# An 8192 x 8192 transpose in two strips: letting regions fill across the seam between the strips

## The chip, the cores and the metric

The kernel runs on one core of a Trainium2 chip. The metric is the device time of one execution in microseconds (us). Every traced execution took about 1.8 us longer than its span, the time from the first to the last instruction. All comparisons of times use runs of state fast. The runs named "look" are single runs, whose state the record calls unknown; only their traces are used.

## The reference

```python
def setup_inputs():
    return {"x": np.random.randn(8192, 8192).astype(np.float32)}

def reference(x):
    return np.transpose(x)
```

268.44 MB are read and 268.44 MB written. There is no arithmetic.

## The kernel before

The matrix is walked in 128 steps: strip 1 (columns 0 to 4095) in 64 chunks of 128 rows, then strip 2. A step loads one chunk of 128 x 4096 values (2 MB), transposes it in 128 x 128 blocks on TensorE, and copies the blocks from PSUM, where TensorE's results land, into *regions* in SBUF, where loads land and stores start. Loads and stores are DMA transfers; SyncEngine issues them into one queue. The output rows of a strip are divided into eight ranges q of 512 rows, and each range has one region open. A region is stored when it holds eight chunks, so that a row of the store is 8 x 128 values = 4096 B. The ranges are staggered: in each step just one region fills, and 2 MB go out beside 2 MB coming in.

At the end of a strip the stagger is cut off: `min(..., CH - 1)` closes all eight regions in step 63, with 8, 7, ... 1 chunks, and strip 2 starts with eight empty regions, the first of which close with 1, 2, ... 8 chunks.

```python
        for t, (s, c) in enumerate(chunks):
            nc.tensor.wait_ge(s_ld[t % NIN], 16 * (t // NIN + 1))
            closing = []
            for q in [(c + k) % NR for k in range(NR)]:
                if q not in window:
                    end = min(c + (q - c) % W, CH - 1)
                    r = free.pop(0)
                    window[q] = (c, end, r)
                    if stored[r]:
                        (nc.scalar, nc.vector)[q % 2].wait_ge(s_st[r], 16 * stored[r])
                ...      # four transposes, one copy, by ScalarE (q even) or VectorE (q odd)
                if c == end:
                    closing.append((q, e, copied[e]))
            for q, e, count in closing:
                ...
                nc.sync.wait_ge(s_cp[e], count)
                ...      # one store of 512 rows on SyncEngine's queue
                st.then_inc(s_st[r], 16)
                free.append(r)
            if t + NIN < len(chunks):
                nc.sync.wait_ge(s_pe, n)
                load(t + NIN)      # NIN = 3 input buffers
```

## Time and profile before

| | |
|---|---|
| time, 3 runs | 1265.46 us median (1265.32 to 1265.71) |
| the profiled run | 1266.41 us, span 1264.6 us |
| chain that ended last | 76% waiting for loads to land, 20% transposes |
| loads | 128 of 2 MB, 23.2 us from issue to landing |
| stores | 142: 114 of 2 MB, 28 shorter ones |

### The profile page before, as it was taken

The numbers are of one execution on the slowest core, as the hardware profiler recorded it, in microseconds if no ns is written. First come the engines' busy times: TensorE is split into PE (matmuls) and PEld (weight loads), VectorE is DVE, ScalarE is ACT, GpSimd is POOL, SyncE is SP. The second block draws the span as 40 slices with busy tenths as digits, with TensorE's granted clock in tenths as the row PEclk, the third lists the DMA queues.
The fourth block names the chain that finished last, engine by engine and source line by source line (L and its number), as shares of the span: only waits on it lengthen the run. The fifth ranks groups of instructions, "written<-read, shape, count | busy, mean of one in ns | idle before, by whom it ended". The sixth has DMA issues, their size and how long they took to land.

```text
span 1264.6 us, 9814 instructions
## 1 busy us (share of the span) xinstructions
PE 741.1 (59%) x4096; PEld 714.3 (56%) x4096; DVE 353.5 (28%) x512; ACT 301.1 (24%) x513; POOL 0.7 (0%) x6
## 2 busy tenths in 40 slices
PE   5555655655556565655556665656556655665651
PEld 5555555655556555655445555656456655665551
DVE  3322322322223222232133322223222222232220
ACT  3222222222222222222122222222222222222220
POOL 0000000000000000000000000000000000000000
PEclk9878777777776868687668778686866777767685
DMA  9999999999999999999999999999999999999998
GB/s 385 426 428 428 430 427 430 430 429 429 429 428 429 430 429 429 430 428 429 428 404 421 430 428 429 431 429 429 429 428 430 429 428 429 430 430 430 428 428 354
DMA packets 39308, 537.51 MB, mean 425 GB/s; under 512 B 4320, under 2 KB 4832, under 8 KB 6240
## 3 DMA queue, kind: packets, MB, share of 16 engines
q1 hardware_dynamic: 39264, 536.89, 99.9%
q8 instruction: 32, 0.52, 0.2%
q14 instruction: 12, 0.10, 0.0%
HBM read 268.44 MB, written 268.44 MB: 425 GB/s over the span
## 4 chain that ended last, share of the span: by engine, by line
DMA 78%; PE 20%; issue 0%; DVE 0%; ACT 0%; SPq 0%; ACTq 0%
DMA in<-in_x_dram 76%; PE ps L132 20%; DMA out_dram<-reg 2%; DVE reg L145 0%; ACT reg L143 0%; SPq L198 0%; SPq L69 0%; ACTq L141 0%
## 5 line engine op out<-in xcount | busy, mean ns | idle before, releaser
L132 PE MATMUL ps<-ident,in 128*128 128x128 f32 x4096 | 741.1, 363 | 495.5 <-DMA in<-in_x_dram 480.9
L132 PEld LDWEIGHTS ps<-ident,in 128*128 128x128 f32 x4096 | 714.3, 219 | 522.0 <-DMA in<-in_x_dram 496.4
L145 DVE COPY reg<-ps 128x512 f32<-128x512 f32 x512 | 353.5, 691 | 883.3 <-PE ps L132 849.3
L143 ACT COPY reg<-ps 128x512 f32<-128x512 f32 x512 | 299.8, 586 | 935.2 <-PE ps L132 904.1
L143 ACT ACT_TABLE_LOAD x1 | 1.3, 1283 | 0.9 <-SPq L69 0.9
L84 POOL TENSOR_SCALAR_AFFINE_SELECT ident<-ident 128x128 f32<-128x128 f32 x1 | 0.3, 293 | 0.2 <-POOL ident L82 0.2
L82 POOL MEMSET ident<- 128x128 f32 x1 | 0.2, 205 | 0.5 <-SPq L69 0.5
L187 POOL MEMSET const-bfloat16-1.0<- 128x1 bf16 x1 | 0.1, 102 | 0.0
L187 POOL MEMSET const-uint8-127<- 128x1 uint8 x1 | 0.1, 102 | 0.0
L187 POOL MEMSET const-float32-0.0<- 128x1 f32 x1 | 0.1, 99 | 0.2 <-issue 0.2
L187 POOL MEMSET const-float32-1.0<- 128x1 f32 x1 | 0.1, 99 | 0.0
## 6 DMA issues: line engine op xcount, KB each, us to landing
in<-in_x_dram SPq DMA_DIRECT2D x128, 2048.0 KB, 23.2
out_dram<-reg SPq DMA_DIRECT2D x114, 2048.0 KB, 22.6
out_dram<-reg SPq DMA_DIRECT2D x4, 1792.0 KB, 19.8
out_dram<-reg SPq DMA_DIRECT2D x4, 1536.0 KB, 19.1
out_dram<-reg SPq DMA_DIRECT2D x4, 1280.0 KB, 19.0
out_dram<-reg SPq DMA_DIRECT2D x4, 1024.0 KB, 17.7
out_dram<-reg SPq DMA_DIRECT2D x4, 768.0 KB, 16.1
out_dram<-reg SPq DMA_DIRECT2D x4, 512.0 KB, 14.2
```

The source lines that it names most:

```text
L82: nc.gpsimd.memset(ident, 0.0).then_inc(s_id, 1)
L84: nc.gpsimd.affine_select(out=ident, in_=ident, compare_op=mybir.AluOpType.not_equal, fill=1.0, base=0, pattern=[[-1, P]], channel_multipl ...
L132: last = nc.tensor.transpose(ps[:, b * P:(b + 1) * P], ins[t % NIN][:, q * B * P + b:(q + 1) * B * P - B + b + 1:B], ident,)
L143: cp = nc.scalar.copy(out=o, in_=i)
L145: cp = nc.vector.tensor_copy(out=o, in_=i)
L187: nc = _bacc.Bacc("TRN2", target_bir_lowering=False, num_devices=1)
```

## The change

A range's last chunks of strip 1 and its first chunks of strip 2 share one region. The stagger goes on across step 64. A region that straddles the seam is stored by two DMAs (7+1 chunks, 6+2, ... 1+7), as its two parts lie in different output rows.

```diff
-                    end = min(c + (q - c) % W, CH - 1)
+                    span = (q - c) % W + 1
                     r = free.pop(0)
-                    window[q] = (c, end, r)
+                    parts = [(s, c, min(c + span, CH))]
+                    if c + span > CH and t + span < len(chunks):
+                        parts.append((s + 1, 0, c + span - CH))
+                    window[q] = (t, r, parts)
 ...
-                if c == end:
+                if t + 1 == t0 + sum(z - a for _, a, z in parts):
                     closing.append((q, e, copied[e]))
             for q, e, count in closing:
 ...
                 nc.sync.wait_ge(s_cp[e], count)
+                base = 0
+                for s_, a, z in parts:
+                    ...      # one store for each part, from its place in the region
```

More of the change, by code (lines that the diff above doesn't have):

```diff
@@ L117 @@
                 if q not in window:
-                    end = min(c + (q - c) % W, CH - 1)
+                    span = (q - c) % W + 1
                     r = free.pop(0)
-                    window[q] = (c, end, r)
+                    parts = [(s, c, min(c + span, CH))]
+                    if c + span > CH and t + span < len(chunks):
+                        parts.append((s + 1, 0, c + span - CH))
+                    window[q] = (t, r, parts)
                     if stored[r]:
                         (nc.scalar, nc.vector)[q % 2].wait_ge(s_st[r], 16 * stored[r])
-                c0, end, r = window[q]
-                rows = (end - c0 + 1) * P
-                view = regs[r][:, :B * rows].rearrange("p (b i) -> p b i", b=B)
+                t0, r, parts = window[q]
+                k = [p[0] for p in parts].index(s)
+                base = B * P * sum(z - a for _, a, z in parts[:k])
+                _, a, z = parts[k]
+                rows = (z - a) * P
+                view = regs[r][:, base:base + B * rows].rearrange("p (b i) -> p b i", b=B)
                 ps = pss[n % NPS]
@@ L138 @@
                 n += 1
-                o = view[:, :, (c - c0) * P:(c - c0 + 1) * P]
+                o = view[:, :, (c - a) * P:(c - a + 1) * P]
                 i = ps.rearrange("p (b i) -> p b i", b=B)
@@ L148 @@
                 bank[(n - 1) % NPS] = (s_cp[e], copied[e])
-                if c == end:
+                if t + 1 == t0 + sum(z - a for _, a, z in parts):
                     closing.append((q, e, copied[e]))
             for q, e, count in closing:
-                c0, end, r = window.pop(q)
-                rows = (end - c0 + 1) * P
-                j0 = s * J + q * B * P
-                dst = out[j0:j0 + B * P, c0 * P:c0 * P + rows]
-                dst = dst.rearrange("(q b) i -> q b i", q=P)
-                nc.sync.wait_ge(s_cp[e], count)
-                if stores:
-                    st = wide_dma(nc, nc.sync, "qSPDynamicHW", dst, regs[r][:, :B * rows])
-                else:
-                    st = nc.sync.dma_start(
-                        out=dst, in_=regs[r][:, :B * rows].rearrange("q (b i) -> q b i", b=B)
-                    )
-                st.then_inc(s_st[r], 16)
-                stores += 1
-                stored[r] += 1
+                t0, r, parts = window.pop(q)
+                nc.sync.wait_ge(s_cp[e], count)
+                base = 0
+                for s_, a, z in parts:
+                    rows = (z - a) * P
+                    j0 = s_ * J + q * B * P
+                    dst = out[j0:j0 + B * P, a * P:a * P + rows]
+                    dst = dst.rearrange("(q b) i -> q b i", q=P)
+                    src = regs[r][:, base:base + B * rows]
+                    base += B * rows
+                    if stores:
+                        st = wide_dma(nc, nc.sync, "qSPDynamicHW", dst, src)
+                    else:
+                        st = nc.sync.dma_start(
+                            out=dst, in_=src.rearrange("q (b i) -> q b i", b=B)
+                        )
+                    st.then_inc(s_st[r], 16)
+                    stores += 1
+                    stored[r] += 1
                 free.append(r)
```

## The prediction

> **What bounds the kernel now.** I read the page first: its busy shares, the 40 slices, the chain that ended last.
>
> ```profile
> span 1264.6 us, 9814 instructions
> PE 741.1 (59%) x4096; PEld 714.3 (56%) x4096; DVE 353.5 (28%) x512; ACT 301.1 (24%) x513; POOL 0.7 (0%) x6
> ...
> GB/s 385 426 428 428 430 427 430 430 429 429 429 428 429 430 429 429 430 428 429 428 404 421 430 428 429 431 429 429 429 428 430 429 428 429 430 430 430 428 428 354
> ...
> q1 hardware_dynamic: 39264, 536.89, 99.9%
> ...
> DMA 78%; PE 20%; issue 0%; DVE 0%; ACT 0%; SPq 0%; ACTq 0%
> ```
>
> No compute engine is busy over 59%; the DMA queue is at 99.9%. The slices (31.6 us each) hold 427 to 431 GB/s nearly everywhere. They fall short in four: 385 and 426 at the start, 354 at the end, and 404 and 421 in slices 21 and 22, which is the seam, where strip 1 (steps 0 to 63) gives way to strip 2. The change works on the seam alone. The page prices it: (429-404)/429 x 31.6 + (429-421)/429 x 31.6 = 1.8 + 0.6 = 2.4 us of lost transfer. That is the first estimate of all that is to be had.
>
> Second, the table by windows, cut where the chain shows loads landing: step 63's at 601.72, step 73's at 702.39; then 5 us pieces inside (columns: busy time of each engine, granted TensorE clock, DMA share, GB/s).
>
> ```profile
> 572.44:601.72 29.28, 17.99 (x96) 17.42 (x96) 8.30 (x12) 7.04 (x12) 0.00 (x0) 0.69 1.01 429
> 601.72:702.39 100.67, 56.60 (x320) 51.88 (x320) 27.19 (x40) 23.17 (x40) 0.00 (x0) 0.72 1.01 417
> 702.39:731.68 29.29, 17.39 (x96) 16.82 (x96) 8.30 (x12) 7.03 (x12) 0.00 (x0) 0.74 1.01 429
> ...
> 635.00:640.00 5.00, 2.22 (x8) 1.42 (x8) 0.03 (x1) 0.59 (x1) 0.00 (x0) 0.50 1.02 386
> 640.00:645.00 5.00, 3.38 (x12) 2.18 (x12) 2.66 (x5) 2.09 (x5) 0.00 (x0) 0.50 1.01 401
> 645.00:650.00 5.00, 0.00 (x0) 0.00 (x0) 1.08 (x2) 0.55 (x1) 0.00 (x0) 0.50 1.03 381
> 650.00:655.00 5.00, 4.20 (x20) 4.20 (x21) 1.17 (x2) 1.17 (x2) 0.00 (x0) 0.50 1.02 428
> 655.00:660.00 5.00, 5.00 (x43) 5.00 (x42) 3.58 (x6) 2.64 (x5) 0.00 (x0) 0.98 1.00 406
> 660.00:665.00 5.00, 3.48 (x29) 3.29 (x28) 2.01 (x3) 2.20 (x5) 0.00 (x0) 1.00 1.00 380
> ```
>
> Three steps take 29.28 us on either side, 9.76 us a step. The ten steps across the seam take 100.67 us, 3.1 us over 97.6. In bytes the loss is 100.67 x (1 - 417/429) = 2.8 us. The DMA share stays at 1.00 or over even where the rate is 381: the engines never show as idle, single packets take longer.
>
> Third, why the rate dips: the SyncEngine's timeline, the waits, and the store latencies in steady state (tile view, 100 to 590 us).
>
> ```profile
> 598.34 0.34 SPq L99 DMA_DIRECT2D in<-in_x_dram  x1
> 603.65 30.76 SPq L28 DMA_DIRECT2D out_dram<-reg  x8
> 634.45 3.65 SPq L99 DMA_DIRECT2D in<-in_x_dram  x1
> 638.15 0.59 SPq L28 DMA_DIRECT2D out_dram<-reg  x1
> 638.79 1.99 SPq L99 DMA_DIRECT2D in<-in_x_dram  x1
> ...
> DVE reg L145 <- DMA out_dram<-reg: 34.0, 6, 17.7
> ACT reg L143 <- DMA out_dram<-reg: 31.1, 4, 13.5
> ...
> DMA to landing us min/median/max: 22.5/22.6/24.1
> ```
>
> At step 63 all eight regions close. The first of their stores takes about 0.6 us to issue, like a normal one (0.54); the fourth takes 8.19, because the queue takes no more. So the next load, issued every 9.8 us otherwise, goes out 36 us after the one before, and step 64 has to wait for regions to be stored (65 us of waits on stores in the whole run, 63.5 of them here). When the stall is over the queue holds only the smallest stores: many rows, few bytes. It runs nearly dry.
>
> **What the Trainium skill says.** (1) "DMA: Bandwidth & Descriptors", Specifications, gives a fabric ceiling of 435 GB/s for the 16 engines. The trace agrees: 429 is 98.6% of it, so steady state has nothing left and only the dips can be regained. (2) The same page, Anatomy of one DMA: the DMA engines do not wait on semaphores, the issuing sequencer does, before dispatch. The trace agrees: the load issued at 634.45 stands behind eight stores issued over 30.76 us. (3) The same page, "Why small descriptors are slow (HBM only)": a fixed overhead per packet. The trace's packet records agree in kind: medians of 611 ns for 16384 B, 315 for 8192, 161 for 4096 and 89 for 2048; the slope from 4096 to 16384 is 36.6 ns per 1000 B, which leaves about 12 to 14 ns fixed.
>
> **The change, part by part.** *Removed*: the burst of eight stores in step 63 and the thin stores of 1 to 7 chunks in steps 64 to 70. *Added*: nothing; the instruction order of the built kernel shows the same 4096 transposes, 512 copies, 128 loads and 142 stores with the same sizes. *Moved*: step 63 stores one full region, and each of steps 64 to 70 stores a pair (7+1, 6+2, ... 1+7 chunks), followed by its load. So every step across the seam moves 2 MB in and 2 MB out, as in steady state.
>
> What is regained: I took the packets that run more than 60 ns over that line (14 ns + 36.4 ns per 1000 B), and added up the excess, divided by 16 engines. In the seam they lie in three clusters: at 638.5 us (13 packets, 0.41 us), 642.4 (50, 0.83) and 658.8 (32, 0.75), 2.0 us together. They coincide with the 5 us windows of 386, 401/381 and 406/380 GB/s. The same sort of cluster stands at the kernel's start (1.7, 15.2, 21.6 us), where the queue is thin too; in steady state such packets come singly, worth some 0.03 us every 40 us. I take the clusters to be a queue that ran dry.
>
> What isn't regained: small packets. The 14 short stores stay, with the same rows. Seven full regions as 16 KB packets would take 7 x 128 x 615 ns / 16 = 34.4 us; the same bytes in the short stores take 35.1 us (half of the totals by packet size of the whole run, as each strip end has a mirror at the start and end). So 0.7 us stay. Check: counted from the packet records, 42.08 MB crossed the seam window, which at 429 GB/s takes 98.1 us, a loss of 2.6 us; less 0.7 leaves 1.9. That agrees with the 2.0 of the clusters.
>
> Beside other work: the second store of a pair costs SyncEngine 0.54 us before the load goes out, but the queue then holds over 20 us of transfers (22.6 us from issue to landing), so it is hidden. Sum: 1265.46 - 1.9 = 1263.5 us.
>
> **The rivals.** *A, the stall was on the path with its full length.* The seam shows over 60 us of waits on stores; step 63 to step 66 takes 49 us where 29.3 would be normal. If all that came back, the time would fall by 20 us or more, to 1245 or, with the waits counted whole, near 1202. Against: the same bytes must still go through a queue that stays at 429 GB/s until 625 us, during the stall; the 20 us lost to loads there are spent on stores, and given back afterwards, when steps 64 to 70 store little (step 66 to 73 takes 51.6 us where 68.3 is normal). *B, a new wait takes its place.* A pair is 1024 rows against a full region's 512, so the queue could fill and SyncEngine stall on issue; and a region is free only when both stores have landed. The reuse margin is small: a store issued at 573.88 lands some 22.6 us later, at 596.5, and the copy that reuses such a region starts at 598.4, 1.9 us of slack. For it: issues did stall at the fourth store above. Against: a stall on a full queue starves nobody, since what is in it, pairs and loads of 2 MB each, is many microseconds of work; a late region holds up the last copy of a step by a microsecond, while TensorE idles 3 to 4 us a step. B leaves between 1263.5 and, if the queue still thins somewhere, 1265.5 (no gain). *C, all of the seam's loss returns*, also the 0.7 us, because slow packets behind small ones are hidden in a full queue: 1265.46 - 2.6 to 3.1, so 1262.4 to 1262.9.
>
> **Range and chances.** The central value is 1263.5. C sets the lower end at 1262.4; half of the gain lost to B, with 0.2 us of run to run spread (1265.32 to 1265.71), sets the upper at 1264.7. Two per cent is 25.3 us, ten times what the seam's dips hold; only rival A reaches that, and it contradicts the byte count. Slower by 2% would need a hang-up that nothing shows. Chances: 0.005 faster, 0.99 within 2%, 0.005 slower.
>
> **What would show each step right or wrong.** Right: slices 21 and 22 at 427 or more; no 5 us window of the seam under about 415; no cluster of slow packets from 600 to 710 us; the waits of copies on stores down from 65 us to a few; SyncEngine's issues at the seam as pairs, one load every 9.8 us; ten steps across the seam in about 98.5 us, not 100.67. Start and end slices unchanged (385, 354). Wrong: if the waits vanish and the dips remain, the dips aren't the thin queue but the short rows; if the rate is flat and the span doesn't fall, the loss has moved elsewhere, first to look at the last slice; a fall of over 5 us would mean that the stall itself was on the path.

## The result

The changed kernel took 1265.7 us median (1265.37 to 1265.88, 6 runs) against 1265.39 us (1265.2 to 1265.8, 6 runs) for the kernel before. The ratio is 1.0002, with an interval from 0.9989 to 1.0015. A ratio is the mean time of one kernel's fast runs over that of the other's in the same rounds, so it isn't quite the ratio of the medians quoted. The time is within 2% of before, as predicted, but outside the predicted range (1262.4 to 1264.7): nothing of the expected 1.9 us appeared. Over all batches, the 42 fast runs of before that served as the comparison have a mean of 1265.62 us (standard deviation 0.51; 1265.64 with the five of before_again) and 11 of the changed kernel 1265.66 (0.17). The difference is 0.04 us, with a standard error of 0.51/√42 and 0.17/√11 taken together, 0.09 us.

Yet the profile of the changed kernel shows what the change was for. From its page:

```profile
span 1263.6 us, 9807 instructions
...
GB/s 385 427 427 430 428 427 430 429 430 429 428 428 428 430 429 429 428 430 429 427 427 412 430 429 428 429 429 429 429 429 429 429 429 427 431 429 429 430 427 351
...
DMA 78%; PE 19%; issue 0%; ACT 0%; SPq 0%; ACTq 0%
```

Slice 21 is mended (427 for 404), slice 22 isn't: 412, where before had 421. The table by windows, cut at the same loads (steps 60, 63, 73 and 76), then 5 us pieces near the end of the seam:

```profile
571.98:601.26 29.28, 16.52 (x96) 15.95 (x96) 8.30 (x12) 7.02 (x12) 0.00 (x0) 0.83 1.01 429
601.26:701.60 100.34, 61.19 (x320) 59.29 (x320) 27.66 (x40) 23.43 (x40) 0.00 (x0) 0.71 1.01 423
701.60:730.88 29.28, 16.59 (x96) 16.02 (x96) 8.29 (x12) 7.03 (x12) 0.00 (x0) 0.79 1.01 429
...
680.00:685.00 5.00, 3.68 (x20) 3.68 (x21) 1.38 (x2) 0.83 (x2) 0.00 (x0) 0.66 1.05 423
685.00:690.00 5.00, 1.66 (x14) 1.46 (x13) 1.38 (x2) 1.51 (x3) 0.00 (x0) 1.00 0.95 349
```

The mean rate over the seam rose from 417 to 423 GB/s. But the ten steps take 100.34 us, only 0.33 less than in the kernel before. There is a new dip, 349 GB/s, at 685 us. The waits of the copies on stores are down from 65 us to 1.7:

```profile
ACT reg L150 <- DMA out_dram<-reg: 1.7, 2, 1.1
```

and SyncEngine's timeline shows a wait in a new place (start, duration, issue):

```profile
606.94 0.34 SPq L99 DMA_DIRECT2D in<-in_x_dram  x1
612.85 1.22 SPq L28 DMA_DIRECT2D out_dram<-reg  x2
...
627.26 6.37 SPq L99 DMA_DIRECT2D in<-in_x_dram  x1
633.90 2.92 SPq L28 DMA_DIRECT2D out_dram<-reg  x2
638.10 5.94 SPq L99 DMA_DIRECT2D in<-in_x_dram  x1
...
678.14 4.42 SPq L99 DMA_DIRECT2D in<-in_x_dram  x1
683.21 0.61 SPq L28 DMA_DIRECT2D out_dram<-reg  x1
686.69 0.33 SPq L99 DMA_DIRECT2D in<-in_x_dram  x1
```

Steps 64 to 70 issue a pair of stores, 1024 rows where a full region has 512, and from 627 to 683 us every load takes 4.4 to 6.4 us to issue instead of 0.34: the queue seems to take no more. (That is inferred from these durations; no view shows how full a queue is.) The dip at 685 us stands just after the last of these.

**A ledger of single DMA engines.** The windows seem to contradict themselves: by the mean rate (100 us at 423 instead of 417 GB/s) the seam should have become 1.4 us shorter, by the landings of loads it became 0.33 shorter. The views of the profile average over 16 DMA engines. The trace has more: each of the 16 engines adds one to a transfer's semaphore when its share has landed, and each of these 16 times is recorded (4320 for the 270 transfers of before), though not the engine it belongs to. From them I made a ledger. In steady state a step's 4 MB take 9.76 us, 0.61 us for each 256 KB chunk. For a load, an engine's *lateness* is its landing time less 0.61 us times the chunks issued up to and with that load. An engine at full rate keeps its lateness; each loss raises it. Here it is for the two kernels' first traces, in us:

```
                     first engine      last engine     mean of 16
before, step 65          3.96             8.77            5.98
before, step 73          7.77            11.84            8.86
after,  step 65          3.83             8.31            5.84
after,  step 73          5.09            11.04            7.64
```

"First" and "last" are the least and most late of the 16 at that load. They are 4.1 to 6.0 us apart. Over the seam of the kernel before, the first engine loses 3.81 us, the mean 2.88 and the last 3.07. In the changed kernel it is 1.26, 1.80 and 2.73. So the change saves the engine that is ahead 2.5 us, the mean 1.1 us, and the engine that is behind 0.34 us. A transfer isn't complete, and the kernel isn't at its end, before the last engine is done: over all 18 executions traced with this ledger, time less the last engine's lateness at the last store is 1252.4 to 1252.6 us. So this one number gives the times of runs between 1263.9 and 1269.7 us to 0.2 us. That isn't a test, as the program waits for its last store and the number is the landing time of that store less a constant; what the ledger adds is where along the run the last engine became late.

What raises the last engine's lateness can be read step by step. In the changed kernel it rises by 1.54 us at step 66's load, by 0.04 to 0.09 at each of steps 67 to 71, and by 0.76 at step 72's. The small ones are the short rows. The first is an instruction fetch: 32 packets of 16 KB on a queue of their own, one about every 39 us, each on a single engine.

```profile
q8 instruction: 32, 0.52, 0.2%
```

(From the page of before; packets, MB, share.) A fetch packet takes about 1.0 us, the packet after it is slow as well, and its engine is 1.3 to 1.5 us later from then on. One of the 16 latenesses rises at a time; followed through the steps between the fetches, they show that successive fetches walk over eight of the 16 engines and come back after eight. That is much of why the engines are apart: in the trace of before the eight that are hit are 11.4 to 13.3 us late at the last load, the other eight 7.7 to 9.9. It isn't all: in before_bf below, with a quarter of the fetches, the engines are still 4.2 us apart at step 65. The fetch at 625 us falls on the engine that is last. In the kernel before, the one at 648 us is the corresponding one in the rotation.

### The profile page after: what moved, and what is told of

Read it like the earlier page. It is cut to its first block, busy times and chain, and to the rows that moved or that the text cites. A ratio compares the mean times of both kernels' runs of the same rounds, so it can differ in the third digit from the quotient of the medians.

```text
span 1263.6 us, 9807 instructions
## 1 busy us (share of the span) xinstructions
PE 748.9 (59%) x4096; PEld 724.9 (57%) x4096; DVE 353.9 (28%) x512; ACT 301.2 (24%) x513; POOL 0.7 (0%) x6
## 2 busy tenths in 40 slices
DMA packets 39308, 537.51 MB, mean 425 GB/s; under 512 B 4320, under 2 KB 4832, under 8 KB 6240
## 4 chain that ended last, share of the span: by engine, by line
DMA 78%; PE 19%; issue 0%; ACT 0%; SPq 0%; ACTq 0%
DMA in<-in_x_dram 78%; PE ps L139 19%; ACT reg L150 0%; SPq L209 0%; SPq L69 0%; ACTq L148 0%
## 5 line engine op out<-in xcount | busy, mean ns | idle before, releaser
L139 PE MATMUL ps<-ident,in 128*128 128x128 f32 x4096 | 748.9, 365 | 486.8 <-DMA in<-in_x_dram 486.8
L139 PEld LDWEIGHTS ps<-ident,in 128*128 128x128 f32 x4096 | 724.9, 219 | 510.7 <-DMA in<-in_x_dram 502.4
```

The lines of the kernel that those rows point to most:

```text
L139: last = nc.tensor.transpose(ps[:, b * P:(b + 1) * P], ins[t % NIN][:, q * B * P + b:(q + 1) * B * P - B + b + 1:B], ident,)
```

## The experiments

Two theories stood at first. **S**: the end is set by the engine that is furthest behind, and the seam's dips cost the others more than that one. **M**: the mean of the engines sets the time, as the prediction had it, and the first trace of before was merely an unlucky one. For each traced run the tables give the loss from step 65's load to step 73's.

### before_again and after_again: the two kernels once more

No edit.

> The kernel before, unchanged, for the noise and for a second trace (its first profiled run took 1266.41 us, 0.95 us over the median of its unprofiled runs). Two theories. S: the end is set by the DMA engine that is furthest behind, and a thin queue costs the engines that are ahead more than that one. M: the mean over the 16 engines sets the time, as the prediction took it, and the first trace was an unlucky one whose dips at the seam are about 1 us larger than usual. Both expect 1265.4 us within 0.4. S expects the seam in the new trace about as in the first: slow packets between 600 and 710 us worth 1.5 to 2.5 us in the mean of the engines, while the last engine loses about 3 us from step 65's load to step 73's, of which about 1.5 us is an instruction fetch that happens to fall on it and 0.6 us the short rows. M expects slow packets worth 1.0 us or less.

> The changed kernel, unchanged. Both theories expect the ratio to before between 0.9995 and 1.0006. S expects in its trace again a mean loss at the seam about 1 us smaller than in the kernel before, but for the last engine a loss of 2.5 to 3.0 us: 1.5 for the instruction fetch, 0.5 for short rows, 0.8 for a new dip at about 683 us. M expects the mean losses of the two new traces to be equal within 0.3 us.

Measured: before 1265.83 us median (1264.88 to 1266.55, 5 runs, ratio 1.0001), changed 1265.65 (1265.47 to 1265.83, ratio 1.0000), both beside 1265.79 of before. Seam losses: before last 3.43, mean 3.04; changed last 2.99, mean 1.91. The mean gains 1.1 us again and the last engine 0.4. S has its numbers; M's equal means do not appear. But the profiled run was again a slow one for its kernel (1266.55), so M's second half was still open.

### before_1mm and after_1mm: fewer instructions, in f32

```diff
-                for b in range(B):
-                    last = nc.tensor.transpose(
-                        ps[:, b * P:(b + 1) * P],
-                        ins[t % NIN][:, q * B * P + b:(q + 1) * B * P - B + b + 1:B],
-                        ident,
-                    )
+                last = nc.tensor.matmul(
+                    ps, lhsT=ident, rhs=ins[t % NIN][:, q * B * P:(q + 1) * B * P],
+                    start=True, stop=True,
+                )
```

> Wrong result on purpose: the four transposes of a group are replaced by one matmul of 512 columns against the identity, so TensorE has a quarter of the instructions and the 16 KB instruction fetches fall from 32 to about 8; data, copies, loads and stores are the same. The trace of before has a fetch about every four steps, each on a single DMA engine, which loses about 1.5 us by it; the last engine is hit four times. S expects three of its four to go: 3.4 to 4.5 us less than before, so 1261 to 1262. M expects the mean of the saved fetch time over 16 engines, 24 x 1.5 / 16 = 2.2 us less, 1263.2.

> The same edit in the changed kernel (wrong result on purpose). With the fetches gone the engines are nearly level, and a thin queue has to hit all of them. S expects the change to pay here what the first prediction said: 1.3 to 2.5 us less than before_1mm, so about 1259.5. M expects the same as before_1mm within 0.4 us, as with the two original kernels.

Measured: 1266.57 us median (1264.9 to 1267.53) and 1266.89 (1266.26 to 1269.68), ratios 1.0004 and 1.0008. Results wrong. Both theories missed. (M's equal times for the pair fit the medians, 0.32 us apart, but the runs of after_1mm differ by 3.4 us.) The fetches fell to 16, not 8, since the page counts 2048 matmuls for 1024 written. The ledger says where the saving went: the steps became slower, the queue ran thin at the start, and the last engine was 9.15 us late at step 13 in before_1mm where the trace of before has 7.41. One thing is worth keeping. SyncEngine's stalls at the seam of before_1mm were as long as in the kernel before (30.26 us for the eight stores), but its last engine lost only 2.01 us there and the mean 0.79, with no cluster of slow loads. A stall need not bring slow loads.

### before_bf and after_bf: fewer instructions and a faster TensorE

```diff
+                last = nc.tensor.matmul(
+                    ps, lhsT=ident.bitcast(mybir.dt.bfloat16)[:, 1:2 * P:2],
+                    rhs=ins[t % NIN].bitcast(mybir.dt.bfloat16)[:, 2 * q * B * P + 1:2 * (q + 1) * B * P:2],
+                    start=True, stop=True,
+                )
```

(in place of the four transposes.)

> Wrong result on purpose: one bf16 matmul of 512 columns on the upper halves of the words in place of four transposes, so TensorE needs far less time than in the f32 variant (whose slower steps thinned the queue at the start) and has a quarter of the instructions: 8 fetches instead of 32. Theory S: eight engines each get one fetch instead of four, the last engine gains about 3 x 1.5 = 4.5 us, and the start does not get worse: 1261 to 1261.8. Theory M: the mean gains 24 x 1.5 / 16 = 2.2 us: 1263.5.

> The same edit in the changed kernel (wrong result on purpose). With the engines within about 2 us of each other. If slow loads in before come from engines so far apart that the first ones run out of work (in the f32 variant with engines 2.5 us apart they were absent from the kernel before), before_bf has none at the seam, and the change gives nothing here either: equal to before_bf within 0.4 us. If the change pays wherever the engines are level, 1.0 us or more less than before_bf.

Measured: 1264.37 us median (1263.65 to 1265.95, ratio 0.9992) and 1265.12 (1263.56 to 1265.59, ratio 0.9993), beside 1265.43. Results wrong. The page of before_bf has the fetches at a quarter:

```profile
q8 instruction: 8, 0.13, 0.0%
```

The gain is about 1 us, against 3.6 to 4.4 expected under S and 2 under M. S was too large because another engine takes the place of one that is relieved: in the traced run (1263.89 us) the last engine ended 2.5 us less late than in the trace of before (11.31 against 13.84), and what the ledger shows beside the fetches is 1.1 us lost at the seam and rises of 0.5 to 1.0 us beside 8 KB packets of another instruction queue. So three quarters of the fetches, with a faster TensorE, are worth about 1 us of the time, not their sum on one engine. And the change does not pay here either: the ratios of the two are the same to 0.0001. That is what the expectation of after_bf asked for, but its reason missed: before_bf was to have no slow loads at the seam, and it has three clusters there (1.1 us in the mean of the engines).

### noseam: what a seam without cost would give

```diff
-        for t, (s, c) in enumerate(chunks):
+        flat = out.rearrange("(j two) i -> j (two i)", two=2)
+        for t in range(len(chunks)):
+            c = t
 ...
-                    end = min(c + (q - c) % W, CH - 1)
+                    end = min(c + (q - c) % W, len(chunks) - 1)
 ...
-                j0 = s * J + q * B * P
-                dst = out[j0:j0 + B * P, c0 * P:c0 * P + rows]
+                j0 = q * B * P
+                dst = flat[j0:j0 + B * P, c0 * P:c0 * P + rows]
```

> Wrong result on purpose: all 128 chunks are treated as one strip, the output seen as 4096 rows of 16384 elements, so no region is cut at step 64, no short rows and no burst; bytes, loads, copies, transposes and both ends of the kernel are as before. It measures all that a seam without cost could give. Theory S (the last engine sets the end): the last engine lost 3.1 to 3.4 us at the seam of before, of which 1.5 is an instruction fetch that stays; 1.6 to 1.9 us less than before, about 1264.0. Theory M (the mean of the engines): it lost 2.9 to 3.0 us, of which 0.2 are fetches; 2.7 us less, about 1263.0. Theory N (typical runs of before lose little at the seam, only the profiled ones do): within 0.5 us of before.

Measured: 1265.39 us median (1264.72 to 1266.77, ratio 1.0002). Result wrong. By its time alone theory N's "within 0.5 us of before" came true, and neither S's 1264.0 nor M's 1263.0. But as a measure of the total it failed: in its one trace the last engine lost more in steps without a seam, perhaps because the output rows are placed otherwise (9.30 us late at step 65, 8.77 in the trace of before; 2.57 after step 73, 2.00 there). Within the seam window it is clean: the last engine lost 0.94 us, the mean 0.26, the first nothing. (The fetch of 1.5 us fell on an engine that was not the last one before it.) So of the last engine's 2.8 us at the seam (mean of five traces, below) 1.8 at most belong to the way the kernel before closes its regions, short rows included. Had the fetch hit the last engine here too, as it does in the kernel before, about 1.3 would be left (an estimate, 2.8 less 1.5).

### before_look1 to before_look3: further traces of the kernel before

No edit; one run each.

> The kernel before once more, only to get further traces of it. Its two traces so far are of runs of 1266.41 and 1266.55 us, above the mean of its 33 runs (1265.65, standard deviation 0.56). If theory N holds (typical runs lose less at the seam than the traced ones), a run at 1265.5 or below shows a loss of the last engine from step 65's load to step 73's of 2.5 us or less, where the two traces have 3.1 and 3.4. If the seam loss is 3.0 to 3.5 whatever the time of the run, the spread comes from elsewhere (start or end).

> As before_look1: a run at 1265.5 us or below with a seam loss of the last engine of 2.5 us or less speaks for N, one of 3.0 to 3.5 against it.

> As before_look1: a run at 1265.5 us or below with a seam loss of the last engine of 2.5 us or less speaks for N, one of 3.0 to 3.5 against it.

With a third trace of the changed kernel (after_look1, whose expectation stands below), the seam losses are, in us:

```
                       time      last    mean    first engine
before (first trace)  1266.41    3.07    2.88    3.81
before_again          1266.55    3.43    3.04    3.39
before_look1          1265.87    2.49    2.21    2.54
before_look2          1265.61    1.96    1.22    1.58
before_look3          1266.66    2.94    2.68    3.50
mean of the five                 2.78    2.41    2.96
after (first trace)   1265.37    2.73    1.80    1.26
after_again           1265.68    2.99    1.91    0.99
after_look1           1265.78    2.69    1.68    1.17
mean of the three                2.80    1.80    1.14
```

The seam of the kernel before costs between 1.2 and 3.0 us in the mean of the engines, by chance, and its time follows. The test written down for theory N (typical runs of before lose less at the seam than the first traced ones) asked for a run at 1265.5 us or below, and none of the three was. The nearest, before_look2 at 1265.61, which is the mean time of the kernel, lost 1.96 us on the last engine, as N expects. Here are its 5 us windows, to be held against those of the first trace in the prediction (386, 401, 381, 428, 406, 380):

```profile
635.00:640.00 5.00, 2.25 (x8) 1.45 (x8) 0.06 (x1) 0.59 (x1) 0.00 (x0) 0.50 1.03 417
640.00:645.00 5.00, 3.33 (x12) 2.19 (x12) 2.51 (x5) 2.05 (x4) 0.00 (x0) 0.50 1.02 417
645.00:650.00 5.00, 0.06 (x1) 0.00 (x0) 1.26 (x3) 0.59 (x1) 0.00 (x0) 0.50 1.03 423
650.00:655.00 5.00, 4.89 (x23) 4.89 (x24) 1.38 (x2) 1.48 (x3) 0.00 (x0) 0.50 1.00 421
655.00:660.00 5.00, 5.00 (x41) 5.00 (x40) 3.37 (x5) 2.51 (x5) 0.00 (x0) 0.93 0.99 417
660.00:665.00 5.00, 3.72 (x31) 3.53 (x31) 2.15 (x4) 2.43 (x5) 0.00 (x0) 1.00 1.01 419
```

The copies wait and TensorE idles just as in the first trace; the deep dips are nearly gone. Both theories hold a part, then. On the average of the traces the change saves the first engine 1.8 us, the mean 0.6 us and the last engine nothing (2.78 against 2.80). One reserve: the five traced runs of before average 1266.22 us, 0.6 above the mean of its other runs, so 2.78 is more than a typical run loses; the three traced runs of the changed kernel, 1265.61, are typical.

### after_swapped: the two stores of a pair in the other order

```diff
-                base = 0
-                for s_, a, z in parts:
+                base = B * P * sum(z - a for _, a, z in parts)
+                for s_, a, z in reversed(parts):
 ...
+                    base -= B * rows
                     src = regs[r][:, base:base + B * rows]
-                    base += B * rows
```

> The changed kernel with the two stores of each pair issued in the other order, strip 2's piece first: 1+7, 2+6 up to 7+1 chunks. If slow loads come from the store of one chunk directly behind a load, the cluster at 683 us goes and one appears at about 621 to 627 us, ahead of step 64's pair. If they come with the end of the stalled issues, the cluster stays at about 683 us. The time is expected at 1265.6 within 0.4 us either way.

Measured: 1266.58 us median (1265.89 to 1266.8, ratio 1.0006), somewhat slower than expected. Of the two places named for the cluster of slow loads, it was at neither: it moved to 644 us (37 packets, 0.90 us in the mean), about one microsecond after a stalled load was out (issued from 637.97 to 643.60), as the one at 683 us in the changed kernel came after a load issued from 678.14 to 682.56. The last engine lost 3.41 us. So the thin store directly behind a load isn't what does it, and neither is the last of the stalls as such.

### after_two_queues: the second store of a pair from ScalarE's queue

```diff
-                for s_, a, z in parts:
+                for k, (s_, a, z) in enumerate(parts):
 ...
+                    if k == 1:
+                        nc.scalar.wait_ge(s_cp[e], count)
+                        if seconds:
+                            st = wide_dma(nc, nc.scalar, "qActDynamicHW", dst, src)
+                        else:
+                            st = nc.scalar.dma_start(
+                                out=dst, in_=src.rearrange("q (b i) -> q b i", b=B)
+                            )
+                        seconds += 1
-                    if stores:
+                    elif stores:
```

> The changed kernel with the second store of each pair issued from ScalarE's own DMA queue, so that SyncEngine's queue holds one store and one load a step as in steady state. If the slow loads at 683 us come from the stalled issues (4 to 6 us per load in the changed kernel), the stalls and the slow loads go, and the last engine loses 0.8 to 1.0 us less: about 1264.8. If they come from a thin store directly behind a load, or from elsewhere, they stay or move, and the time stays at 1265.6 within 0.4.

It was run again later, with further traces, for its time:

> The version with two queues once more, for its time and a second trace. If the first measurement was no accident: 0.3 to 0.7 us below before, 1265.0 to 1265.3, and a seam loss of the last engine of 1.9 to 2.2 us without a cluster of slow loads.

> The changed kernel once more for a third trace. Seam loss of the last engine (step 65's load to step 73's) 2.6 to 3.1 us with a cluster of slow loads at 683 us, as in its first two traces; the mean of the engines 1.7 to 2.0 us.

Measured: 1265.05 us median (1264.82 to 1265.31, ratio 0.9996), and in the second batch, two_queues_again, 1265.13 (1264.8 to 1265.31, ratio 0.9997). after_look1 behaved as expected (table above; its mean of 1.68 lies just under the range). By the comparison within the rounds both are as before (intervals 0.9984 to 1.0009). SyncEngine's timeline of after_two_queues in the seam:

```profile
622.68 0.55 SPq L28 DMA_DIRECT2D out_dram<-reg  x1
626.80 0.33 SPq L99 DMA_DIRECT2D in<-in_x_dram  x1
634.63 0.55 SPq L28 DMA_DIRECT2D out_dram<-reg  x1
638.13 0.33 SPq L99 DMA_DIRECT2D in<-in_x_dram  x1
```

No issue is stalled, and no cluster of slow loads is left. In both traces the last engine loses 2.01 us at the seam (mean 0.95 and 0.99, first 0.65): 1.5 for the fetch and 0.5 for short rows. Its ten runs have a mean of 1265.09 us, 0.57 less than the changed kernel's 1265.66 (standard error 0.08) and 0.52 less than before's 1265.62 (0.10); by the last engine's losses 2.80 - 2.01 = 0.8 us was to be expected. Pooled over all batches, then, this version, whose results are correct, beats both kernels, if only by 0.04%.

The Trainium skill says, in "DMA: Bandwidth & Descriptors", Issuing engines are not separate DMA queues, that DMAs issued from several engines run on the same 16 DMA engines and that this only saves the sequencer's time of issue. These runs agree as far as they show it: each transfer still lands in 16 shares. They don't agree that only time of issue is saved: the stalls of 4.4 to 6.4 us are gone, but so are the slow loads, and the last engine loses 0.8 us less.

### split_mid and split_mid_two_queues: the same stalls far from the seam

Is it the stalled issue that brings the slow loads of the changed kernel (theory Q), or something of the seam (theory A)? In the kernel before, with its seam as it was, I split the full regions that close in steps 38 to 44 into two stores of 4 chunks. That gives the queue 1024 rows a step where nothing else happens. The second kernel takes the second halves to ScalarE's queue with the edit shown for after_two_queues. (The diff is against the changed kernel; its first two lines bring back the seam of before. The lines that find a chunk's part and close a region, changed to match, are left out.)

```diff
                     parts = [(s, c, min(c + span, CH))]
-                    if c + span > CH and t + span < len(chunks):
-                        parts.append((s + 1, 0, c + span - CH))
+                    if 38 <= t + span - 1 <= 44:
+                        parts = [(s, c, c + W // 2), (s, c + W // 2, c + W)]
 ...
```

> The kernel before with its seam as it was, and the full regions that close in steps 38 to 44, in the middle of strip 1, each stored as two halves of 4 chunks (right result). It gives SyncEngine's queue the same 1024 rows a step that the pairs of the changed kernel give it, but far from the seam. In the traces of before and after nothing happens to the last engine from step 37's load to step 50's (0.00 us). Theory Q (the stalled issues of loads behind so many rows bring the slow loads, as at 683 us in the changed kernel): loads stall 4 to 6 us in issue, and the last engine loses 1.1 to 1.6 us there: 0.4 to 0.6 for the rows of 2 KB and 0.7 to 1.0 from a cluster of slow loads at the end of the stretch. Theory A (the slow loads belong to the seam itself, to its addresses or its mixture of sizes): stalls, but only 0.4 to 0.6 us lost.

> The same, the second half of each region stored from ScalarE's own queue. Theory Q: no stall, no cluster, only 0.4 to 0.6 us lost by the last engine from step 37's load to step 50's. Theory A: the same as split_mid within 0.3 us.

Measured: split_mid 1267.68 us median (1266.36 to 1269.24, ratio 1.0017), split_mid_two_queues 1266.58 (1265.97 to 1267.55, ratio 1.0009), beside 1265.51. In split_mid, loads stall in issue as at the changed seam:

```profile
392.84 5.66 SPq L99 DMA_DIRECT2D in<-in_x_dram  x1
398.55 3.49 SPq L28 DMA_DIRECT2D out_dram<-reg  x2
402.66 6.97 SPq L99 DMA_DIRECT2D in<-in_x_dram  x1
```

and in split_mid_two_queues none does:

```profile
392.78 0.34 SPq L99 DMA_DIRECT2D in<-in_x_dram  x1
401.37 0.55 SPq L28 DMA_DIRECT2D out_dram<-reg  x1
405.69 0.34 SPq L99 DMA_DIRECT2D in<-in_x_dram  x1
```

From step 37's load to step 50's, the last engine loses 3.63 us in split_mid and 0.66 in split_mid_two_queues; the mean loses 1.74 and 1.05 (0.36 in the first trace of before, which is fetches). Clusters of slow packets stand at about 398, 408 and 419 us in split_mid, none in the other. Theory Q stands, with a larger size than I gave it (1.1 to 1.6), and theory A falls: the same rows, stalls and slow loads appear without a seam, and both go with a second queue. This rests on one trace of each kernel; their times, 1266.4 to 1269.2 and 1266.0 to 1267.6 us, overlap. A rival is left as well: the second queue takes away the stalls and also changes how loads and stores lie side by side in the queues, and no run takes away the stalls alone. What a stalled issue does to loads that lie in the queue already is left open. before_1mm shows that stalls do not always have that effect, and no run here shows the mechanism.

## Why the prediction was wrong, point by point

- **What bounds the kernel** was right: the DMA engines, at about 429 GB/s outside the seam and the two ends (and outside the split steps of the last two kernels), in every trace. It wasn't sharp enough. "Perfetto Trace Analysis", What "DMA-bound" means, in the Trainium skill lists specific DMA engines as one thing a kernel can be bound on. Here it is the engine that is furthest behind at the end.
- **"added up the excess, divided by 16 engines"** is the step that failed. It gives the mean of the engines (2.0 us for the clusters, 2.6 less 0.7 by bytes), and as a mean it holds: the three clusters are gone. But it isn't what the end waits for. The last engine lost about as much as the mean in that trace, 3.07 us, but of something else: some 1.5 us was an instruction fetch, which no change at the seam removes, and some 0.5 short rows, which the prediction rightly left in. About 1 us was left to gain there instead of 1.9. The prediction had seen the fetches' slow packets, "worth some 0.03 us every 40 us": that is 0.5 us on one engine, divided by 16.
- **The one trace** was the second error. The profiled run was 0.95 us slower than the median of its kernel, and the seam was where. Five traces give a loss on the last engine of 1.96 to 3.43 us, 2.78 in the mean. After fetch and short rows 0.8 us is left, and less in a typical run, since the traced runs of before were slow ones: the version with two queues gains 0.52.
- **"Beside other work"** held that a second store costs only 0.54 us of issue, hidden under a full queue. The queue was full, and that was the trouble: loads stalled 4.4 to 6.4 us in issue, and slow loads at 683 us cost the last engine 0.76, 0.99 and 0.74 us in three traces (0.85 in the mean of the engines in the first). That is what the change had gained. Taking the stall away with a second queue brought back 0.57 us.
- **Rival B** named the right event (the queue fills and SyncEngine stalls) and then argued it away, since a full queue starves nobody. Its upper end, "1265.5 (no gain)", was where the time came out; the range stopped half way there. The other half of B, late regions, did not happen: 1.7 us of waits on stores.
- **Rival A** was rightly dismissed: the waits of copies on stores fell from 65 us to 1.7 and the time did not move.
- **"I take the clusters to be a queue that ran dry"** isn't supported. In the changed kernel the cluster at 683 us hits a load that had been in the queue for 10 us; in before_look2 nearly the same issues brought almost no slow loads (0.5 us in the mean, 2.1 in the first trace). What makes a packet slow stays open.
- **The signs to look for**: the waits, the pairs, and the unchanged start (385 GB/s) came as said. The flat rate, the absent clusters and ten steps in 98.5 us did not. The case listed as "the loss has moved elsewhere" is the nearest to what happened, within the seam.
- **Slips** that change nothing: five slices fall short and not four (385, 426, 404, 421, 354), and the medians of the packets leave 11 to 15 ns fixed, not 12 to 14.

## What to carry to other kernels

In a kernel bound by DMA, ask which of the 16 engines ends last and what made it late; a mean rate prices a dip for an engine that does not set the end. For gains of a microsecond compare the profiled run with the other runs first, and take several traces. When a change puts more and shorter rows on one queue, look at the durations of the issues themselves: if they grow from 0.3 us to several, as here, try two queues; it was worth 0.57 us in this kernel.

## What the Trainium skill lacked or had wrong

- "DMA: Bandwidth & Descriptors", Queues, rings and completion order, does not say that issuing stalls when the queue is full, or at what fill. Here the fourth of eight stores of 512 rows took 8.19 us to issue, and loads behind pairs of 512-row stores took 4.4 to 6.4 us instead of 0.34. With the second stores on ScalarE's queue they took 0.33.
- The same page's Issuing engines are not separate DMA queues says that issuing from several engines saves only the sequencer's time. Here it also took away slow loads: the last engine's loss at the seam fell from 2.80 to 2.01 us and the time by 0.57 (1265.66 to 1265.09).
- "Runtime: NRT & Kernel Launch", Instruction fetch mechanics, has the 16 KB blocks and their own DMA queue, as here (32 packets), but calls the cost mostly hidden, and no page says which engines carry them. In this kernel they ran in turn on eight of the 16 engines, and each put its engine back by 1.3 to 1.5 us; with that and other losses the engines were 4.1 to 6.0 us apart, and a transfer's last share landed that much after its first.
- "Perfetto Trace Analysis", Identifying the Most-Contended Engine, advises total DMA throughput over occupancy and then to find which DMA resource binds. It doesn't say how to tell which of the 16 engines that is, and neither measure shows the last one: at the seam the mean gained 1.1 us between the two first traces and the last engine 0.34.
